# A fused low-rank update on one core: TensorE's program written as one loop, the turned group at a fixed place, last loads of 8 and 4 tiles

## The chip, the core and the metric

The kernel runs on one core of one Trainium2 chip. The core has TensorE (PE, matrix products), VectorE (DVE), ScalarE (ACT), GpSimd (POOL) and SyncE (SP, which here only issues DMAs and passes signals on). Data moves between the chip's memory (HBM) and the core's memory (SBUF) by DMAs, which 16 DMA engines of the core carry out together. Matrix products land in PSUM. The metric is the time of one execution on the device, in microseconds (us); lower is better.

## The reference

```
batch, seq, d_model, r = 16, 512, 768, 16
x: [16, 512, 768] f32    A: [768, 16]    B: [16, 768]    scale = 0.5

lora = np.matmul(np.matmul(x, A), B)
return (x + scale * lora).astype(np.float32)
```

As a matrix, x has 8192 rows of 768. The inner dimension of the update is 16, so there is little arithmetic, while all of x is read (25.2 MB) and a result of the same size is written.

## The kernel before

**Tiles, groups, parts.** A tile is 128 rows of x by 768, and there are 64. All of them stay in SBUF in one buffer, `x_all`, and the sums are written in place there. Four tiles are a group (16 groups, 0 to 15); two tiles are a pair. The tiles lie in five parts of 8, 16, 16, 12 and 12 (`PARTS`). A part is stored by one DMA: stores 0 to 4 follow groups 1, 5, 9, 12 and 15. The loads are the list `LOADS` (part, first tile, tiles): loads 0 to 7 have 2, 6, 8, 8, 16, 12, 10 and 2 tiles. In `x_all` the last part's place also serves as room for the constants while they are prepared (`lent`), so loads 6 and 7, which fill that place, can only start when its lodgers are gone.

**The stages of a group g.**

1. *Narrowing* (L209 to L223): ScalarE copies two tiles of the group to 16 bit, GpSimd the other two. Group 1 is narrowed whole by ScalarE.
2. *Turning* (L276 to L278): VectorE transposes the narrowed group in blocks of 32x32.
3. *Projecting* (L312 to L327): 24 matmuls on TensorE multiply by A, in a block-diagonal form `w_bd`. The second raises `s_taken`, the last raises `s_y`.
4. *Spreading* (L261 to L265): ScalarE multiplies the small result by the scale and writes it into a block-diagonal `y_bd`, of which there are two.
5. *Raising* (L329 to L345): 8 matmuls multiply by B (`b_mm`), four for each pair of tiles, into two PSUM buffers `lora`.
6. *Summing* (L280 to L287): VectorE adds the PSUM buffer to `x_all`, one instruction for a pair.

**Places.** The narrowed group lies in one fixed buffer `xn` (group 1: in lent room, `xn_1`). The turned group moves (`turn_of`, L106): the last two tiles' place of `x_all` for groups 0 and 2 to 7 (`xt_a`), lent room for group 1 (`xt_1`), in place in `xn` for groups 8 to 10 (`PLACE`), and from group 11 on the first two tiles' place, `xt_c`, which is free once store 0 has landed (`s_out0`).

**Orders.** Each engine has its own program, and semaphores tie them together.

- TensorE (L347 to L383): it first copies B to four row blocks (L349 to L353), then projects groups 0 and 1, then for each g: raise g, project g + 2. Because the address of the turned group changes, the `while` loop (L368) writes this as a hardware loop of three passes for g = 0 to 5, four steps written out, a loop of two passes, and the last two raises written out. As the program's order lists them, 322 matmuls stand in it; 514 are executed.
- VectorE (L289 to L307): turn 0, turn 1, then for each g: turn g + 2, sum the two pairs of g.
- ScalarE (L254 to L267): narrow, make `b_mm`, then for each g: spread g, narrow its half of g + 2.
- GpSimd (L225 to L252): clears buffers, prepares `w_bd`, then narrows its halves.
- SyncE (L181 to L207): loads 0 and 1, A, B, loads 2 to 5; waits for the first raise (`s_lora`) and issues load 6; waits for the sums of parts 0 and 1 and for the projection of group 7 (`s_y`, L200) and issues load 7; waits until load 6 has landed (L202) and issues stores 0 and 1; then waits for the sums of each further part and issues its store. All these DMAs go through one queue, q1.

Of the kernel before, what the change touches and what calls it, by code (L numbers as in the profile page):

```python
# [9 lines left out]
MM_DT = mybir.dt.float16  # L10
# [3 lines left out]
PARTS = [8, 16, 16, 12, 12]  # L14


GROUP = 4

SUB = 2
# [2 lines left out]


PLACE = range(8, 11)

APART = 4
# [4 lines left out]
def kernel(  # L34
# [9 lines left out]
    fp32 = mybir.dt.float32  # L44
    P = 128
    Q = 32
    NQ = P // Q
# [3 lines left out]
    T, D = x2.shape  # L51
    R = A.shape[1]
    NC = D // 64
    NG = sum(PARTS) // GROUP
    PAIRS = GROUP // 2
# [4 lines left out]
    def sb(name, shape, dtype):  # L60
        return nc.alloc_sbuf_tensor(name, shape, dtype).ap()
# [6 lines left out]
    ROOM = sum(PARTS)  # L68
    x_all = sb("x_sb", [P, ROOM, D], fp32)
    w_bd = sb("w_bd", [P, NC, 2, P], MM_DT)  # L70
    b_mm = sb("b_mm", [P, D], MM_DT)
    xn = sb("xn", [P, GROUP, D], MM_DT)
    y_bd = sb("y_bd", [P, 2, GROUP, P], MM_DT)
    lora = [ps(f"lora_ps{i}", [P, 2, D]) for i in range(2)]
    y_ps = [ps(f"ps_yt{i}", [P, GROUP, Q]) for i in range(2)]
# [5 lines left out]
    def lent(n, dtype=fp32):  # L81
        n = n if dtype is fp32 else n // 2
        taken[0], first = taken[0] + n, taken[0]
        assert taken[0] <= (PARTS[-1] - SUB) * D
        v = late[:, ds(first, n)]
        return v if dtype is fp32 else v.bitcast(dtype)

# [3 lines left out]
    b_half = lent(D, MM_DT)  # L91
    pick = lent(P, MM_DT).rearrange("p (b r) -> p b r", b=NQ)
    w_one = lent(NC * 2 * R, MM_DT)[0:Q].rearrange("i (c k r) -> i c k r", c=NC, k=2)
    xn_1 = lent(GROUP * D, MM_DT).rearrange("p (s d) -> p s d", s=GROUP)
    xt_1 = lent(GROUP * D, MM_DT).rearrange("p (s d) -> p s d", s=GROUP)

    def turned_in(t):
        v = x_all[:, ds(t, SUB), :].rearrange("p s d -> p (s d)").bitcast(MM_DT)
        return v.rearrange("p (s d) -> p s d", s=GROUP)

    xt_a, xt_c = turned_in(ROOM - SUB), turned_in(0)

    def narrow_of(g):
        return xn_1 if g == 1 else xn

    def turn_of(g):  # L106
        return xt_1 if g == 1 else xt_a if g < PLACE[0] else xn if g in PLACE else xt_c

    sems = []

    def sem(name):
        sems.append(nc.alloc_semaphore(name))
        return sems[-1]
# [17 lines left out]
    def tiles(t, n):  # L131
        return x_all[:, ds(t % ROOM, n), :]

    LOADS = [
        (0, 0, 2), (0, 2, 6), (1, 0, 8), (1, 8, 8), (2, 0, 16), (3, 0, 12), (4, 0, 10), (4, 10, 2)
    ]
    s_load = [sem(f"s_load{k}") for k in range(len(LOADS))]

# [6 lines left out]
    s_ready, s_brows, s_pick = sem("s_ready"), sem("s_brows"), sem("s_pick")  # L145
    s_wv = sem("s_wv")
    s_w, s_bh, s_bp, s_bm = sem("s_w"), sem("s_bh"), sem("s_bp"), sem("s_bm")
    s_first, s_narrow, s_taken = sem("s_first"), sem("s_narrow"), sem("s_taken")
    s_turned = [sem(f"s_turned{h}") for h in range(2)]
    s_y, s_spread, s_lora = sem("s_y"), sem("s_spread"), sem("s_lora")  # L150


    s_free = [[sem(f"s_free{h}_{p}") for p in range(PAIRS)] for h in range(2)]
# [12 lines left out]
    def on_sync(e):  # L166
        def load(k):
            ld = LOADS[k]
            e.dma_start(out=held(*ld), in_=memory(x2, *ld)).then_inc(s_load[k], 16)

        def summed(k):
            e.wait_ge(s_sum, k + 1)
            if STORED[k] + 1 < NG:

                e.sem_inc(s_free[STORED[k] % 2][PAIRS - 1], 1)

        def store(k, done):
            st = STORES[k]
            e.dma_start(out=memory(out2, *st), in_=held(*st)).then_inc(done, 16)

        load(0)  # L181
        load(1)
        e.wait_ge(s_ready, 1)
        blocks = A.rearrange("(c e) r -> c (e r)", e=64)
        for c in range(SETS):
            e.dma_start(  # L186
                out=a_rows[c : SET * SET : SET, :], in_=blocks[ds(c * SET, SET), :]
            ).then_inc(s_a, 16)
        e.wait_ge(s_brows, 1)
        e.dma_start(out=b_rows[0 : R * APART : APART, :], in_=B).then_inc(s_b, 16)  # L190
        for k in range(2, len(LOADS) - 2):
            load(k)

        for p in range(PAIRS):
            e.sem_inc(s_free[1][p], 1)
        e.wait_ge(s_lora, 1)
        load(len(LOADS) - 2)
        summed(0)
        summed(1)
        e.wait_ge(s_y, PLACE[0])  # L200
        load(len(LOADS) - 1)
        e.wait_ge(s_load[len(LOADS) - 2], 16)  # L202
        store(0, s_out0)
# [7 lines left out]
    def narrowed(e, copy, g, first, n=SUB):  # L211
        t = g * GROUP + first
        for k in dict.fromkeys(load_of(t + k) for k in range(n)):
            if (e, k) not in here:
                here.add((e, k))
                e.wait_ge(s_load[k], 16)
        if g - 1 in PLACE:
            e.wait_ge(s_y, g)
        elif g > 1:
            e.wait_ge(s_taken, g if g > 2 else 1)  # L220
        ins = copy(out=narrow_of(g)[:, ds(first, n), :], in_=tiles(t, n))  # L221

        ins.then_inc(s_narrow if g > 1 else s_first if g or first else s_a, 1)  # L223

    def on_gpsimd(e):  # L225
        e.memset(a_rows[0:Q], 0.0).then_inc(s_ready, 1)  # L226
# [19 lines left out]
        for b in range(NQ - 1):  # L246
# [4 lines left out]
        for g in range(2, NG):  # L251
            narrowed(e, e.tensor_copy, g, SUB)  # L252

    def on_scalar(e):  # L254
        narrowed(e, e.copy, 0, SUB)
        narrowed(e, e.copy, 1, 0, GROUP)
        e.wait_ge(s_bp, 1)
        e.copy(out=b_mm, in_=lora[0][:, 0, :]).then_inc(s_bm, 1)
        narrowed(e, e.copy, 2, 0)
        for g in range(NG):  # L260
            e.wait_ge(s_y, g + 1)  # L261
            for b in range(NQ):
                q = ds(b * Q, Q)
                last = e.mul(out=y_bd[q, g % 2, :, q], in_=y_ps[g % 2][q, :, :], mul=sc)  # L264
            last.then_inc(s_spread, 1)  # L265
            if 1 <= g < NG - 2:
                narrowed(e, e.copy, g + 2, 0)  # L267

    def on_vector(e):
        e.wait_ge(s_a, SETS * 16 + 1)  # L270
        e.transpose(  # L271
            out=a_t[0:Q].rearrange("i k r c -> i (k r) c"),
            in_=a_rows[0:Q].rearrange("c (i k r) -> c (k r) i", k=2, r=R),
        ).then_inc(s_ready, 1)

        def turned(g):  # L276
            ts = [v.bitcast(fp32) for v in (turn_of(g), narrow_of(g))]
            e.transpose(out=ts[0], in_=ts[1]).then_inc(s_turned[g % 2], 1)  # L278

        def summed(g, p):  # L280
            xs = tiles(g * GROUP + 2 * p, 2)
            e.wait_ge(s_lora, g * PAIRS + p + 1)
            ins = e.tensor_tensor(out=xs, in0=xs, in1=lora[p % 2], op=mybir.AluOpType.add)  # L283
# [5 lines left out]
        for g in range(2):  # L289
            e.wait_ge(s_first, g + 1)  # L290
            turned(g)
            if g == 0:
                b = NQ - 1
                e.wait_ge(s_w, 1)
                e.tensor_copy(
                    out=w_bd[ds(b * Q, Q), :, :, ds(b * Q, R)], in_=w_one
                ).then_inc(s_wv, 1)
        for g in range(NG):
            if g + 2 < NG:
                if g + 2 == PLACE[-1] + 1:  # L300
                    e.wait_ge(s_out0, 16)
                elif g + 2 not in PLACE:
                    e.wait_ge(s_y, g + 2 if g else 1)
                e.wait_ge(s_narrow, 2 * (g + 1))
                turned(g + 2)
            for p in range(PAIRS):
                summed(g, p)  # L307

    def on_tensor(e):


        def projected(h, xt):  # L312
# [15 lines left out]

        def raised(h, p):  # L329
            if p == 0:  # L330
                e.wait_ge(s_spread, 1)
            free = s_free[1 - h][p]
            e.wait_ge(free, 1)
            t = lora[p % 2]
# [5 lines left out]
                        start=True, stop=True,  # L340
                    ))
            if p == 0:
                mms[2].then_inc(s_spread, -1)
            mms[1].then_inc(free, -1)
            mms[-1].then_inc(s_lora, 1)  # L345

# [7 lines left out]
        last.then_inc(s_bp, 1)  # L354
        e.wait_ge(s_w, NQ)
        e.wait_ge(s_wv, 1)
        projected(0, turn_of(0))
        projected(1, turn_of(1))
        e.wait_ge(s_bm, 1)

        def step(g):
            for p in range(PAIRS):
                raised(g % 2, p)
            if g + 2 < NG:
                projected(g % 2, turn_of(g + 2))

        g = 0
        while g < NG:  # L368

            n = 1  # L370
            while g + 2 * n + 3 < NG and all(
                turn_of(t + 2) is turn_of(g + 2) for t in range(g, g + 2 * n + 2)
            ):
                n += 1
            same = g + 3 < NG and turn_of(g + 2) is turn_of(g + 3)
            if same and n > 1 and g % 2 == 0:
                with e.Fori(0, n):
                    step(g)
                    step(g + 1)
                g += 2 * n  # L380
            else:
                step(g)
                g += 1  # L383

    on_sync(nc.sync)
    on_gpsimd(nc.gpsimd)
# [47 lines left out]
```

## Time and profile before

| what | value |
|---|---|
| median of 3 runs | 125.72 us (125.69 to 125.72) |
| the profiled execution's own time | 125.75 us |
| its span | 124.0 us, so 1.75 us of its time lie outside the span |
| mean granted TensorE clock | 0.88 of full speed |
| moved by DMA | 50.48 MB, 407 GB/s over the span |
| busy shares | VectorE 67%, TensorE 45%, ScalarE 35%, GpSimd 24% |

How to read it: a busy share is an engine's busy time over the span. In the view of DMA queues, a row gives the queue, its packets, the MB they moved and the time they took as a share of 16 engines times the length of the stretch asked for. A packet is counted in the stretch in which it *starts*, with all the time it took; in a short stretch the share can so be over 100%, and for a single packet share x length x 16 gives how long that packet took. At the end of each load and store, every DMA engine sends one packet of 4 bytes that signals its own part as done; the count "under 512 B" so shows when each of the 16 engines came to the end of a transfer.

### The profile page before, as it was taken

To read this page: it belongs to the slowest core of one execution; us is meant where nothing else is said; L and a number is where in the kernel's file an instruction comes from. 1 tells how busy PE (TensorE), PEld (TensorE's weight loads), DVE (VectorE), ACT (ScalarE), POOL (GpSimd) and SP (SyncE) were. 2 spreads that over 40 slices of the span, in tenths; PEclk is the share of its full clock that TensorE was granted. 3 is DMA by queue.
4 is the path that set the end of the run, shared out by engine and by line. 5 is a ranking of instruction groups with operands and counts; after the bars stand their busy time and mean duration, and the time that the engine had idled before them with its cause. 6 is when DMAs were issued, how large, how long until landed. Compare 5 with 4: busy or idle time off the path is not lost.

```text
span 124.0 us, 1339 instructions
## 1 busy us (share of the span) xinstructions
PE 55.5 (45%) x514; PEld 36.5 (29%) x514; DVE 82.8 (67%) x50; ACT 43.9 (35%) x82; POOL 29.2 (24%) x30
## 2 busy tenths in 40 slices
PE   0000287947647249947647249757647520000000
PEld 0000086634415046534415044534515200000000
DVE  0003954999999099999999199999999991000000
ACT  4003929827430555716174334726533000000000
POOL 7722604404400421404044031413400000000000
PEclk9999999999999955999999985999999998555555
DMA  3999999999899899899699999699799999999980
GB/s 67 436 416 468 420 428 444 412 492 508 354 397 448 381 500 452 379 416 466 266 389 494 397 508 460 291 508 476 333 460 494 416 393 393 404 512 416 404 381 12
DMA packets 1932, 50.48 MB, mean 407 GB/s; under 512 B 236, under 2 KB 236, under 8 KB 520
## 3 DMA queue, kind: packets, MB, share of 16 engines
q1 hardware_dynamic: 1928, 50.43, 95.4%
q8 instruction: 2, 0.03, 0.1%
q14 instruction: 2, 0.02, 0.0%
HBM read 25.26 MB, written 25.17 MB: 407 GB/s over the span
## 4 chain that ended last, share of the span: by engine, by line
DMA 51%; DVE 22%; issue 4%; SPq 2%; ACT 2%; POOL 1%; PE 1%; POOLq 0%
DMA x_sb<-in_x_dram 43%; DVE x_sb L283 15%; DMA out_dram<-x_sb 8%; DVE x_sb L278 7%; SPq L186 2%; ACT xn L221 1%; ACT y_bd L264 1%; POOL x_sb L226 1%; PE lora_ps L338 1%; SPq L190 0%; POOLq L429 0%; SPq L164 0%
## 5 line engine op out<-in xcount | busy, mean ns | idle before, releaser
L283 DVE TENSOR_TENSOR x_sb<-x_sb,lora_ps 128x1536 f32<-128x1536 f32 x32 | 54.0, 1732 | 0.0
L221 ACT CAST xn<-x_sb 128x1536 f16<-128x1536 f32 x15 | 22.1, 1472 | 45.0 <-PE ps_yt L317 27.1
L221 POOL CAST xn<-x_sb 128x1536 f16<-128x1536 f32 x15 | 22.0, 1466 | 54.1 <-PE ps_yt L317 43.0
L338 PE MATMUL lora_ps<-b_mm,y_bd 128*128 128x512 f16 (+1 forms) x128 | 27.7, 346 | 12.9 <-DVE x_sb L283 8.6
L317 PE MATMUL ps_yt<-x_sb,w_bd 128*128 128x128 f16 x312 | 23.1, 237 | 16.4 <-DVE x_sb L278 13.8
L317 PEld LDWEIGHTS ps_yt<-x_sb,w_bd 128*128 128x128 f16 x312 | 21.3, 105 | 20.8 <-issue 20.6
L278 DVE STREAM_TRANSPOSE x_sb<-xn 128x1536 f32<-128x1536 f32 x12 | 21.2, 1763 | 8.6 <-PE ps_yt L317 3.1
L264 ACT ACTIVATE y_bd<-ps_yt 32x128 f16<-32x128 f32 x64 | 17.2, 268 | 5.8 <-PE ps_yt L317 4.9
L338 PEld LDWEIGHTS lora_ps<-b_mm,y_bd 128*128 128x128 f16 x128 | 11.0, 102 | 26.1 <-DVE x_sb L283 11.5
L271 DVE STREAM_TRANSPOSE x_sb<-x_sb 32x1024 f32<-32x1024 f32 x1 | 1.9, 1948 | 11.3 <-DMA x_sb<-in_A_dram 11.3
L350 PE MATMUL lora_ps<-x_sb 128*128 128x512 f16 (+1 forms) x2 | 0.8, 504 | 12.5 <-POOL x_sb L239 12.5
L317 PE MATMUL ps_yt<-xn,w_bd 128*128 128x128 f16 x72 | 4.6, 218 | 3.0 <-DVE xn L278 3.0
L317 PEld LDWEIGHTS ps_yt<-xn,w_bd 128*128 128x128 f16 x72 | 4.2, 96 | 4.0 <-issue 4.0
L278 DVE STREAM_TRANSPOSE xn<-xn 128x1536 f32<-128x1536 f32 x3 | 5.3, 1772 | 0.0
L350 PEld LDWEIGHTS lora_ps<-x_sb 128*128 128x128 f16 x2 | 0.1, 104 | 12.5 <-issue 12.5
L221 ACT CAST x_sb<-x_sb 128x3072 f16<-128x3072 f32 x1 | 2.7, 2746 | 0.0
L239 POOL CAST x_sb<-x_sb 128x768 f16<-128x768 f32 x1 | 0.8, 827 | 4.6 <-DMA x_sb<-in_B_dram 4.6
L278 DVE STREAM_TRANSPOSE x_sb<-x_sb 128x1536 f32<-128x1536 f32 x1 | 1.8, 1778 | 0.0
L221 ACT ACT_TABLE_LOAD x1 | 1.3, 1283 | 0.9 <-SPq L164 0.9
L247 POOL COPY w_bd<-x_sb 32x384 f16<-32x384 f16 x3 | 1.5, 499 | 0.2
L229 POOL MEMSET w_bd<- 128x1536 f32 x1 | 1.4, 1372 | 0.0
L226 POOL MEMSET x_sb<- 32x1024 f32 x1 | 0.9, 942 | 0.5 <-SPq L164 0.5
(11 smaller groups left out, 4.2 us busy)
## 6 DMA issues: line engine op xcount, KB each, us to landing
out_dram<-x_sb SPq DMA_DIRECT2D x2, 6144.0 KB, 25.0
out_dram<-x_sb SPq DMA_DIRECT2D x2, 4608.0 KB, 20.6
x_sb<-in_x_dram SPq DMA_DIRECT2D x2, 3072.0 KB, 17.4
x_sb<-in_x_dram SPq DMA_DIRECT2D x1, 6144.0 KB, 35.9
x_sb<-in_x_dram SPq DMA_DIRECT2D x1, 4608.0 KB, 46.4
x_sb<-in_x_dram SPq DMA_DIRECT2D x1, 3840.0 KB, 39.6
out_dram<-x_sb SPq DMA_DIRECT2D x1, 3072.0 KB, 9.4
x_sb<-in_x_dram SPq DMA_DIRECT2D x1, 2304.0 KB, 9.8
```

Of the source, the lines that this page charges most:

```text
L186: e.dma_start(out=a_rows[c : SET * SET : SET, :], in_=blocks[ds(c * SET, SET), :]).then_inc(s_a, 16)
L221: ins = copy(out=narrow_of(g)[:, ds(first, n), :], in_=tiles(t, n))
L226: e.memset(a_rows[0:Q], 0.0).then_inc(s_ready, 1)
L229: e.memset(w_bd.rearrange("p c k m -> p (c k m)").bitcast(fp32), 0.0)
L247: e.tensor_copy(out=w_bd[ds(b * Q, Q), :, :, ds(b * Q, R)], in_=w_one).then_inc(s_w, 1)
L264: last = e.mul(out=y_bd[q, g % 2, :, q], in_=y_ps[g % 2][q, :, :], mul=sc)
L271: e.transpose(out=a_t[0:Q].rearrange("i k r c -> i (k r) c"), in_=a_rows[0:Q].rearrange("c (i k r) -> c (k r) i", k=2, r=R),).then_inc(s_r ...
L278: e.transpose(out=ts[0], in_=ts[1]).then_inc(s_turned[g % 2], 1)
L283: ins = e.tensor_tensor(out=xs, in0=xs, in1=lora[p % 2], op=mybir.AluOpType.add)
L317: mm = e.matmul(y_ps[h], w_bd[:, c, k, :], xv[:, :, c, :, k], start=(m == 0), stop=(m == MMS - 1),)
L338: mms.append(e.matmul(t[:, k, ds(n0, w)], y_bd[:, h, 2 * p + k, :], b_mm[:, ds(n0, w)], start=True, stop=True,))
L350: last = e.matmul(lora[0][:, 0, ds(n0, w)], pick.rearrange("p b r -> p (b r)"), b_half[:, ds(n0, w)], start=True, stop=True,)
```

## The change

The narrowed group and the turned group change roles. The turned group has one fixed buffer, `xt`, in all groups. The narrowed group moves (`narrow_of`): the last two tiles' place of `x_all` for groups 0 to 7 (`xn_a`), `xt` itself for groups 8 to 10 (turned in place), and the first two tiles' place from group 11 on (`xn_c`). With it:

- The lent buffers `xn_1` and `xt_1` are gone. Group 1 is narrowed half by ScalarE, half by GpSimd like the others, after group 0's projection has begun.
- The waits for a place stand at the narrowing: groups 8 to 10 wait for the projection before (`s_y`), group 11 waits until store 0 has landed, the others wait for `s_taken`. Every turn but the first waits for the projection before it.
- TensorE's program is one hardware loop of eight passes: project an even group, raise the group before, project an odd group, raise the group before; one raise follows the loop. In the first pass the raise before group 0 works on a cleared `y_bd`, and nobody reads what it writes. SyncE opens the semaphores that this empty raise waits for; counts of `s_lora` are two higher. 74 matmuls stand in the program; 522 are executed. TensorE now waits for `b_mm` ahead of group 0's projection.
- `s_narrow` and `s_spread` are split in two, for even and odd groups.
- Loads 6 and 7 have 8 and 4 tiles. Load 6 waits for the third count of `s_lora`, load 7 for `s_taken` of group 7 in place of its `s_y`.

```diff
-    xt_a, xt_c = turned_in(ROOM - SUB), turned_in(0)
+    xn_a, xn_c = narrow_in(ROOM - SUB), narrow_in(0)
 
     def narrow_of(g):
-        return xn_1 if g == 1 else xn
-
-    def turn_of(g):
-        return xt_1 if g == 1 else xt_a if g < PLACE[0] else xn if g in PLACE else xt_c
+        return xn_a if g < PLACE[0] else xt if g in PLACE else xn_c
...
-        (0, 0, 2), (0, 2, 6), (1, 0, 8), (1, 8, 8), (2, 0, 16), (3, 0, 12), (4, 0, 10), (4, 10, 2)
+        (0, 0, 2), (0, 2, 6), (1, 0, 8), (1, 8, 8), (2, 0, 16), (3, 0, 12), (4, 0, 8), (4, 8, 4)
...
-        for p in range(PAIRS):
-            e.sem_inc(s_free[1][p], 1)
-        e.wait_ge(s_lora, 1)
+        for h in range(2):
+            for p in range(PAIRS):
+                e.sem_inc(s_free[h][p], 1)
+        e.sem_inc(s_spread[1], 1)
+        e.wait_ge(s_lora, PAIRS + 1)
         load(len(LOADS) - 2)
         summed(0)
         summed(1)
-        e.wait_ge(s_y, PLACE[0])
+        e.wait_ge(s_taken, PLACE[0])
         load(len(LOADS) - 1)
...
-        if g - 1 in PLACE:
+        if g in PLACE:
             e.wait_ge(s_y, g)
-        elif g > 1:
-            e.wait_ge(s_taken, g if g > 2 else 1)
+        elif g == PLACE[-1] + 1:
+            e.wait_ge(s_out0, 16)
+        elif g:
+            e.wait_ge(s_taken, g)
...
         narrowed(e, e.copy, 0, SUB)
-        narrowed(e, e.copy, 1, 0, GROUP)
         e.wait_ge(s_bp, 1)
         e.copy(out=b_mm, in_=lora[0][:, 0, :]).then_inc(s_bm, 1)
-        narrowed(e, e.copy, 2, 0)
+        narrowed(e, e.copy, 1, 0)
...
+        for t in range(1, NG + 2):
+            if t < NG:
+                e.wait_ge(s_y, t)
+                e.wait_ge(s_narrow[t % 2], 2 * ((t + 1) // 2))
+                turned(t)
+            if t > 1:
+                for p in range(PAIRS):
+                    summed(t - 2, p)
...
-        projected(0, turn_of(0))
-        projected(1, turn_of(1))
         e.wait_ge(s_bm, 1)
...
+        with e.Fori(0, NG // 2):
+            for h in range(2):
+                projected(h)
+                for p in range(PAIRS):
+                    raised(1 - h, p)
+        for p in range(PAIRS):
+            raised(1, p)
```

More of the change, by code (lines that the diff above doesn't have):

```diff
@@ L71 @@
     b_mm = sb("b_mm", [P, D], MM_DT)
-    xn = sb("xn", [P, GROUP, D], MM_DT)
+    xt = sb("xt", [P, GROUP, D], MM_DT)
     y_bd = sb("y_bd", [P, 2, GROUP, P], MM_DT)
@@ L83, in lent @@
         taken[0], first = taken[0] + n, taken[0]
-        assert taken[0] <= (PARTS[-1] - SUB) * D
+        assert taken[0] <= (PARTS[-1] - GROUP) * D
         v = late[:, ds(first, n)]
@@ L93, with narrow_in @@
     w_one = lent(NC * 2 * R, MM_DT)[0:Q].rearrange("i (c k r) -> i c k r", c=NC, k=2)
-    xn_1 = lent(GROUP * D, MM_DT).rearrange("p (s d) -> p s d", s=GROUP)
-    xt_1 = lent(GROUP * D, MM_DT).rearrange("p (s d) -> p s d", s=GROUP)
-    def turned_in(t):
+    def narrow_in(t):
         v = x_all[:, ds(t, SUB), :].rearrange("p s d -> p (s d)").bitcast(MM_DT)
         return v.rearrange("p (s d) -> p s d", s=GROUP)
-    xt_a, xt_c = turned_in(ROOM - SUB), turned_in(0)
+    xn_a, xn_c = narrow_in(ROOM - SUB), narrow_in(0)
     def narrow_of(g):
-        return xn_1 if g == 1 else xn
-    def turn_of(g):
-        return xt_1 if g == 1 else xt_a if g < PLACE[0] else xn if g in PLACE else xt_c
+        return xn_a if g < PLACE[0] else xt if g in PLACE else xn_c
     sems = []
@@ L147 @@
     s_w, s_bh, s_bp, s_bm = sem("s_w"), sem("s_bh"), sem("s_bp"), sem("s_bm")
-    s_first, s_narrow, s_taken = sem("s_first"), sem("s_narrow"), sem("s_taken")
+    s_first, s_taken = sem("s_first"), sem("s_taken")
+    s_narrow = [sem(f"s_narrow{h}") for h in range(2)]
     s_turned = [sem(f"s_turned{h}") for h in range(2)]
-    s_y, s_spread, s_lora = sem("s_y"), sem("s_spread"), sem("s_lora")
+    s_y, s_lora = sem("s_y"), sem("s_lora")
+    s_spread = [sem(f"s_spread{h}") for h in range(2)]
     s_free = [[sem(f"s_free{h}_{p}") for p in range(PAIRS)] for h in range(2)]
@@ L216, in narrowed @@
                 e.wait_ge(s_load[k], 16)
-        if g - 1 in PLACE:
+        if g in PLACE:
             e.wait_ge(s_y, g)
-        elif g > 1:
-            e.wait_ge(s_taken, g if g > 2 else 1)
+        elif g == PLACE[-1] + 1:
+            e.wait_ge(s_out0, 16)
+        elif g:
+            e.wait_ge(s_taken, g)
         ins = copy(out=narrow_of(g)[:, ds(first, n), :], in_=tiles(t, n))
-        ins.then_inc(s_narrow if g > 1 else s_first if g or first else s_a, 1)
+        ins.then_inc(s_narrow[g % 2] if g else s_first if first else s_a, 1)
     def on_gpsimd(e):
@@ L250, in on_gpsimd @@
             e.wait_ge(s_w, b + 2)
-        for g in range(2, NG):
+        for g in range(1, NG):
             narrowed(e, e.tensor_copy, g, SUB)
@@ L264, in on_scalar @@
                 last = e.mul(out=y_bd[q, g % 2, :, q], in_=y_ps[g % 2][q, :, :], mul=sc)
-            last.then_inc(s_spread, 1)
-            if 1 <= g < NG - 2:
+            last.then_inc(s_spread[g % 2], 1)
+            if g + 2 < NG:
                 narrowed(e, e.copy, g + 2, 0)
@@ L276, in turned @@
         def turned(g):
-            ts = [v.bitcast(fp32) for v in (turn_of(g), narrow_of(g))]
+            ts = [v.bitcast(fp32) for v in (xt, narrow_of(g))]
             e.transpose(out=ts[0], in_=ts[1]).then_inc(s_turned[g % 2], 1)
@@ L281, in summed @@
             xs = tiles(g * GROUP + 2 * p, 2)
-            e.wait_ge(s_lora, g * PAIRS + p + 1)
+            e.wait_ge(s_lora, (g + 1) * PAIRS + p + 1)
             ins = e.tensor_tensor(out=xs, in0=xs, in1=lora[p % 2], op=mybir.AluOpType.add)
@@ L287, in summed, with projected @@
                 ins.then_inc(s_free[g % 2][p], 1)
[L289 to L307, printed above, removed]
+        e.wait_ge(s_first, 1)
+        turned(0)
+        b = NQ - 1
+        e.wait_ge(s_w, 1)
+        e.tensor_copy(
+            out=w_bd[ds(b * Q, Q), :, :, ds(b * Q, R)], in_=w_one
+        ).then_inc(s_wv, 1)
+        for t in range(1, NG + 2):
[6 more added lines that the diff above has]
+                    summed(t - 2, p)
     def on_tensor(e):
-        def projected(h, xt):
+        def projected(h):
             xv = xt.rearrange("p s (c j k) -> p s c j k", c=NC, k=2)
@@ L330, in raised @@
             if p == 0:
-                e.wait_ge(s_spread, 1)
+                e.wait_ge(s_spread[h], 1)
             free = s_free[1 - h][p]
@@ L342, in raised @@
             if p == 0:
-                mms[2].then_inc(s_spread, -1)
+                mms[2].then_inc(s_spread[h], -1)
             mms[1].then_inc(free, -1)
@@ L356, in on_tensor @@
         e.wait_ge(s_wv, 1)
-        projected(0, turn_of(0))
-        projected(1, turn_of(1))
         e.wait_ge(s_bm, 1)
[L361 to L383, printed above, removed]
+        with e.Fori(0, NG // 2):
[5 more added lines that the diff above has]
+            raised(1, p)
     on_sync(nc.sync)
```

## The prediction

> **What bounds the kernel now.** I read the page first: engines, DMA queues, the chain and the DMA issues.
>
> ```profile
> span 124.0 us, 1339 instructions
> PE 55.5 (45%) x514; PEld 36.5 (29%) x514; DVE 82.8 (67%) x50; ACT 43.9 (35%) x82; POOL 29.2 (24%) x30
> ...
> DMA packets 1932, 50.48 MB, mean 407 GB/s; under 512 B 236, under 2 KB 236, under 8 KB 520
> ...
> q1 hardware_dynamic: 1928, 50.43, 95.4%
> q8 instruction: 2, 0.03, 0.1%
> q14 instruction: 2, 0.02, 0.0%
> out_dram<-x_sb SPq DMA_DIRECT2D x2, 4608.0 KB, 20.6
> ```
>
> The DMA engines work 95.4% of the span in q1; VectorE, the busiest engine, works 67%. Then SyncE's timeline over the whole span, and VectorE's last row there:
>
> ```profile
> 61.65 41.44 SPq L179 DMA_DIRECT2D out_dram<-x_sb  x5
> 92.69 10.04 DVE L283 TENSOR_TENSOR x_sb<-x_sb,lora_ps 128x1536 f32<-128x1536 f32 x6
> ```
>
> The sums end at 102.73, and the last store is issued right then (61.65 + 41.44 = 103.09 is the end of that issue). It needs some 20 us to land, since the two stores of 4608 KB take 20.6 in the middle, though their data alone need 4.72 MB / 407 GB/s = 11.6. So it stands in the queue for about 9 us: the compute is early, and the time is the DMA engines' time. What counts is where they stand idle and which of the 16 is last. The first is in the windows at 61.4 (columns: window, length, VectorE busy, TensorE clock, DMA share, GB/s):
>
> ```profile
> 61.40:62.40 1.00, 1.00 (x2) 1.00 0.15 61
> 62.40:63.40 1.00, 0.98 (x2) 1.00 0.97 406
> ```
>
> In one microsecond they move 61 GB/s in place of 406, so 0.85 us is lost. The chain of waits and the view of DMA queues, asked for the stretches 59 to 60.2, 60.2 to 61.1 and 61.15 to 61.2, tell why:
>
> ```profile
> 22.01 39.62 DMA x_sb<-in_x_dram
> 61.65 9.37 DMA out_dram<-x_sb
> ```
>
> ```profile
> DMA packets 60, 0.30 MB, mean 251 GB/s; under 512 B 15, under 2 KB 15, under 8 KB 59
> ```
>
> ```profile
> DMA packets 58, 0.36 MB, mean 396 GB/s; under 512 B 0, under 2 KB 0, under 8 KB 58
> ```
>
> ```profile
> DMA packets 4, 0.02 MB, mean 369 GB/s; under 512 B 1, under 2 KB 1, under 8 KB 4
> ```
>
> Load 6 lands at 22.01 + 39.62 = 61.63 and store 0 is issued at 61.65 (L202). But 15 of the 16 engines had closed load 6 by 60.2 (15 small packets); the last one does so at 61.15 to 61.2, about 1 us later. The 15 then have only load 7 left, 2 tiles, or 0.79 MB / 407 GB/s = 1.9 us, and run dry before store 0 reaches them.
>
> The second place is the end, in the same view from 120.7 to 121.2, 121.2 to 121.6, 121.6 to 122 and 122 to 122.7:
>
> ```profile
> DMA packets 12, 0.00 MB, mean 0 GB/s; under 512 B 12, under 2 KB 12, under 8 KB 12
> ```
>
> ```profile
> DMA packets 2, 0.04 MB, mean 92 GB/s; under 512 B 1, under 2 KB 1, under 8 KB 1
> ```
>
> ```profile
> DMA packets 2, 0.00 MB, mean 0 GB/s; under 512 B 2, under 2 KB 2, under 8 KB 2
> ```
>
> ```profile
> DMA packets 1, 0.00 MB, mean 0 GB/s; under 512 B 1, under 2 KB 1, under 8 KB 1
> ```
>
> Twelve engines are done by 121.2, then one, two, and a last one after 122; from the last two packets' places I put it at 122.6, some 1.5 us behind the twelve.
>
> What makes one engine late? The instruction queues, q8 and q14. In the view of queues, the stretches 32.3 to 32.4, 33.3 to 33.4, then 75.4 to 75.405, 77.7 to 77.9, 78.7 to 78.8, and at last 95 to 96.5:
>
> ```profile
> q1 hardware_dynamic: 4, 0.20, 450.4%
> q8 instruction: 1, 0.02, 65.6%
> ```
>
> ```profile
> q1 hardware_dynamic: 1, 0.05, 145.1%
> ```
>
> ```profile
> q1 hardware_dynamic: 1, 0.05, 3016.2%
> ```
>
> ```profile
> q8 instruction: 1, 0.02, 30.0%
> ```
>
> ```profile
> q1 hardware_dynamic: 1, 0.05, 136.6%
> ```
>
> ```profile
> q14 instruction: 1, 0.01, 1.3%
> ```
>
> An ordinary packet of 49 KB takes 4.504 x 1.6 / 4 = 1.80 us. The q8 packet at 32.3 takes 0.656 x 1.6 = 1.05, and the data packet that begins when it ends takes 1.451 x 1.6 = 2.32, so 0.52 too long: one engine loses 1.57 at most, and about 1 us is what load 6's last engine lacks. The q8 packet at 77.8 takes 0.300 x 3.2 = 0.96, with a data packet ahead of 30.162 x 0.08 = 2.41 and one behind of 1.366 x 1.6 = 2.19: 0.96 + 0.61 + 0.39 = 1.96 lost on one engine, about the 1.5 by which the last engine is late. That these packets hit just these engines is my inference; the sizes and the times fit.
>
> **The change, part by part.** *Instructions.* 322 matmuls, each with its weight load, stand in TensorE's program now, and 74 then. The others execute 82 (ScalarE), 50 and 30 instructions, so only TensorE's program is long enough to be fetched twice in blocks of q8's size; I take q8 to be its. A program of under a quarter of the length needs no second fetch, or one. Value: the late one goes, the early one may stay. Bounds: both stay (0), both go.
>
> The Trainium skill (Runtime: NRT & Kernel Launch, Instruction fetch mechanics) says that programs are fetched in blocks of 16 KiB by the sequencer's own queue; the trace agrees, with q8's 0.03 MB in 2 packets. By it 2 x 74 instructions, at 256 to a block, would fit one block, and both packets would go: an end at 121.1, and the same sum.
>
> *Last loads.* Load 6 has 8 tiles in place of 10, so it lands 2 x 0.393 MB / 407 GB/s = 1.9 us earlier, at 59.7 even with its late engine. Behind it load 7 has 3.9 us of work in place of 1.9; both together end where they did, so the first engines still run dry at about 61.4, and store 0, issued 1.9 us earlier, is there by then (the row at 62.40 shows it at work 0.75 us after its issue). The idle 0.85 us goes, for each engine but the late one. That one had none, and was among the twelve that end by 121.2 (the hole gave the others its delay).
>
> *The sum.* Ends now: twelve by 121.2, the others at about 121.5, 122, 122 and 122.6. Without the hole the ordinary ones end by 120.3 and the two of 122 at 121.1; those I leave late, since q14's packet (0.013 x 1.5 x 16 = 0.31 and its neighbours) lies in that stretch and belongs to programs that hardly change. If the early q8 packet stays, its engine ends at 121.2. The last end goes from 122.6 to 121.1 or 121.2 (120.8 if the two come out a little better): 1.4 to 1.8 less, and I take 1.7. 125.75 - 1.7 = 124.05, rounded to **124.0**; the median of the runs shown, 125.72, is the same within 0.03.
>
> *The start.* TensorE's timeline, then VectorE's, ScalarE's and VectorE's again:
>
> ```profile
> 15.90 4.35 PE L317 MATMUL ps_yt<-x_sb,w_bd 128*128 128x128 f16 x48 [2.58 <-POOL w_bd L247]
> ...
> 21.16 1.47 PE L338 MATMUL lora_ps<-b_mm,y_bd 128*128 128x512 f16 x8 [0.91 <-ACT y_bd L264]
> ...
> 47.66 2.49 PE L338 MATMUL lora_ps<-b_mm,y_bd 128*128 128x512 f16 x8
> ```
>
> ```profile
> 20.28 1.78 DVE L278 STREAM_TRANSPOSE x_sb<-xn 128x1536 f32<-128x1536 f32 x1 [3.12 <-PE ps_yt L317]
> ```
>
> ```profile
> 41.62 1.47 ACT L221 CAST xn<-x_sb 128x1536 f16<-128x1536 f32 x1 [6.44 <-DMA x_sb<-in_x_dram]
> ```
>
> ```profile
> 43.22 1.78 DVE L278 STREAM_TRANSPOSE x_sb<-xn 128x1536 f32<-128x1536 f32 x1 [2.82 <-POOL xn L221]
> ```
>
> Group 1 now follows group 0: its narrowing begins once group 0's projection has (15.9 + 0.4), ends at 17.8, its turn waits for that projection's end (15.9 + 2.2 = 18.1) and ends at 19.9; the empty raise (8 matmuls, 1.47 to 2.49 us by the rows at 21.16 and 47.66) lies beside it. Projection 1 starts at about 20.2, group 2 is narrowed from 20.6 to 22.1 and turned at 22.1, in place of 20.28: 1.8 us late. At 43.22 VectorE now waits 2.82 us for group 6, whose load lands at 41.62; the delay is swallowed there, with 1.0 us to spare. Without this cover, it would come out of the 9 us that the last store stands in the queue.
>
> Load 7 is issued behind the sums of group 5; SyncE's timeline has it at
>
> ```profile
> 53.39 0.33 SPq L169 DMA_DIRECT2D x_sb<-in_x_dram  x1
> ```
>
> a stretch that the delay doesn't reach; it must be there by 59. The other groups keep the order turn, sum, sum at 5.0 us a group. Groups 8 to 10 are narrowed one projection (1.5 us) later and still end when VectorE comes free, as groups 9 to 11 do now. `b_mm` comes earlier than `w_bd`, so its new place costs nothing.
>
> *Group 11.* Its turn waits for store 0 now:
>
> ```profile
> 71.04 1.78 DVE L278 STREAM_TRANSPOSE x_sb<-xn 128x1536 f32<-128x1536 f32 x1 [2.63 <-DMA out_dram<-x_sb]
> ```
>
> After the change the narrowing waits for it, so the turn comes 1.5 us (one CAST of 1.47) later, and all that follows on VectorE with it. Behind the wait on ScalarE stands the spreading of group 10, on GpSimd nothing that is due; the raise of group 10 comes after projection 11 anyway. The last store is issued at 104.3 in place of 102.8. The stretch 109 to 112.5 shows all 16 engines closing store 3:
>
> ```profile
> DMA packets 52, 1.33 MB, mean 379 GB/s; under 512 B 16, under 2 KB 16, under 8 KB 16
> ```
>
> So store 4 is wanted from 109 on at the earliest, 108.15 without the hole; less 0.75 for the way from issue to work, there are 3.1 us to spare. Stores 2 and 3, behind the sums of groups 9 and 12, have as much or more. Cost: nothing, up to that bound.
>
> **The rivals.**
>
> 1. *Only the hole goes.* A late instruction packet stays (TensorE's, or one of the tail's) and one engine ends 2 us behind the ordinary ones: 120.3 + 1.5 to 2.0 = 121.8 to 122.3, so 125.0. For it: q8's owner is inferred. Or the hole stays and the late packet goes: 122 in place of 122.6, 125.1.
> 2. *Nothing.* The early and the late packet both stay and meet on one engine. The early one's engine ends by 121.2 though it never idled; the late loss of 1.5 to 1.96 on top gives 122.6 or a little more: 125.7.
> 3. *Slower: the loop fetches itself again.* The loop is jumped back to seven times. If each pass fetched a block, 8 packets of q8 at 1.57 to 1.96 would fall on the 16 engines; it decides once two of them meet on one engine late: 120.3 + 2 x 1.96 = 124.2, or 127.3 in all; all eight on one would give 135. Against it: the program now makes five passes in two loops, and q8 shows two packets. The Trainium skill says at the same place that a taken branch out of the two pages held forces a fetch before execution goes on; of that these rows show nothing.
>
> **How the numbers follow.** Forecast (both terms, 123.6 to 124.5): 0.60. Rival 1: 0.20. Rival 2: 0.06. Rival 3, 0.10, and with it any compute delay of more than the 3.1 us to spare at store 4. Better still (all late engines in line, 120.3, so 123.4 and below): 0.04. The forecast and rival 1 hold 0.80: the range is 123.4 to 125.2. Within 0.2% (0.25 us, about what a measurement of this kernel can tell from no change): 0.06; faster 0.84; slower 0.10.
>
> **What would show it.** Right: no q8 row, or one early; GB/s near 406 through 59 to 63; store 0 issued before 60; the last of the small packets near 121; group 11's turn 1 to 1.5 us behind store 0's landing, the last sum near 104. Wrong: several q8 packets, a new stretch of few GB/s behind store 0, 3 or 4 (the sums are late), or a last engine 2 us behind the rest.

## The result, and the profile after

The changed kernel takes 123.91 us (median; 123.87 to 124.01) against 125.70 for the kernel before beside it: a ratio of 0.9861, 95% interval 0.9844 to 0.9878. 124.0 had been forecast. The profiled execution took 123.87 us, 1.88 less than that of before, and its span went from 124.0 to 122.1. The page of the changed kernel, in the lines that answer to those of before:

```profile
span 122.1 us, 1371 instructions
PE 56.6 (46%) x522; PEld 37.0 (30%) x522; DVE 82.8 (68%) x50; ACT 42.8 (35%) x82; POOL 30.7 (25%) x31
...
DMA packets 1930, 50.45 MB, mean 413 GB/s; under 512 B 236, under 2 KB 236, under 8 KB 392
...
q1 hardware_dynamic: 1928, 50.43, 96.7%
q14 instruction: 2, 0.02, 0.0%
...
out_dram<-x_sb SPq DMA_DIRECT2D x1, 3072.0 KB, 11.4
```

The same data moves in less time, and no row for q8 is left: both of TensorE's 16 KB packets are gone, not only the late one. The windows of the changed kernel at the place of the hole (window, length, VectorE busy, clock, DMA share, GB/s) show 516 GB/s where there were 61:

```profile
61.40:62.40 1.00, 1.00 (x1) 0.50 1.21 516
62.40:63.40 1.00, 0.56 (x1) 0.50 1.14 492
```

SyncE's timeline of the changed kernel over the whole span gives the issue of load 7, and then the five stores, the first at 58.69 in place of 61.65:

```profile
52.84 0.33 SPq L164 DMA_DIRECT2D x_sb<-in_x_dram  x1
58.69 45.11 SPq L174 DMA_DIRECT2D out_dram<-x_sb  x5
```

The view of DMA queues of the changed kernel, for the stretches 57.4 to 58.3 (load 6), and then 119.3 to 119.9, 119.9 to 120.5 and 120.5 to 120.8 (store 4); the count under 512 B is that of the engines that close the transfer:

```profile
DMA packets 39, 0.28 MB, mean 314 GB/s; under 512 B 16, under 2 KB 16, under 8 KB 16
...
DMA packets 14, 0.04 MB, mean 62 GB/s; under 512 B 13, under 2 KB 13, under 8 KB 13
...
DMA packets 1, 0.00 MB, mean 0 GB/s; under 512 B 1, under 2 KB 1, under 8 KB 1
...
DMA packets 2, 0.00 MB, mean 0 GB/s; under 512 B 2, under 2 KB 2, under 8 KB 2
```

All 16 engines close load 6 within 0.9 us; before, one was a microsecond behind. At the end 13 are done by 119.9 and the last by 120.8, where 12 had been done by 121.2 and the last after 122. VectorE in the changed kernel's timeline, at groups 2, 6, 10, 11 and the last sums:

```profile
22.72 1.78 DVE L277 STREAM_TRANSPOSE xt<-x_sb 128x1536 f32<-128x1536 f32 x1 [2.13 <-POOL x_sb L221]
...
42.69 1.76 DVE L277 STREAM_TRANSPOSE xt<-x_sb 128x1536 f32<-128x1536 f32 x1
...
63.96 1.78 DVE L277 STREAM_TRANSPOSE xt<-xt 128x1536 f32<-128x1536 f32 x1 [1.00 <-POOL xt L221]
...
71.74 1.78 DVE L277 STREAM_TRANSPOSE xt<-x_sb 128x1536 f32<-128x1536 f32 x1 [2.69 <-POOL x_sb L221]
...
93.39 10.04 DVE L282 TENSOR_TENSOR x_sb<-x_sb,lora_ps 128x1536 f32<-128x1536 f32 x6
```

VectorE starts later, turns group 11 at 71.74 in place of 71.04 and ends at 103.43 in place of 102.73, in a kernel that is 1.8 us faster: the compute does not set the time.

### The profile page after: what moved, and what is told of

It reads as the page before. It is cut to its first block, busy times and chain, and to the rows that moved or that the text cites. A ratio compares the mean times of both kernels' runs of the same rounds, so it can differ in the third digit from the quotient of the medians.

```text
span 122.1 us, 1371 instructions
## 1 busy us (share of the span) xinstructions
PE 56.6 (46%) x522; PEld 37.0 (30%) x522; DVE 82.8 (68%) x50; ACT 42.8 (35%) x82; POOL 30.7 (25%) x31
## 4 chain that ended last, share of the span: by engine, by line
DMA 45%; DVE 25%; issue 5%; PE 4%; POOL 4%; SPq 1%; POOLq 0%; DVEq 0%
DMA x_sb<-in_x_dram 29%; DVE x_sb L282 15%; DMA out_dram<-x_sb 9%; DVE xt L277 9%; DMA x_sb<-in_A_dram 6%; PE ps_yt L312 3%; DVE x_sb L270 2%; POOL w_bd L247 1%; POOL x_sb L221 1%; SPq L181 1%; POOL x_sb L226 1%; POOL x_sb L241 1%; PE lora_ps L333 1%; POOLq L406 0%; DVEq L298 0%
## 5 line engine op out<-in xcount | busy, mean ns | idle before, releaser
L312 PE MATMUL ps_yt<-xt,w_bd 128*128 128x128 f16 x384 | 27.8, 233 | 19.7 <-DVE xt L277 17.0
L333 PE MATMUL lora_ps<-b_mm,y_bd 128*128 128x512 f16 (+1 forms) x136 | 28.7, 340 | 12.2 <-DVE x_sb L282 8.6
L312 PEld LDWEIGHTS ps_yt<-xt,w_bd 128*128 128x128 f16 x384 | 25.2, 103 | 25.7 <-issue 25.7
L221 ACT CAST x_sb<-x_sb 128x1536 f16<-128x1536 f32 x13 | 19.1, 1472 | 35.9 <-PE ps_yt L312 18.9
L221 POOL CAST x_sb<-x_sb 128x1536 f16<-128x1536 f32 x13 | 19.1, 1468 | 40.3 <-PE ps_yt L312 29.2
L277 DVE STREAM_TRANSPOSE xt<-x_sb 128x1536 f32<-128x1536 f32 x13 | 22.9, 1763 | 8.3 <-POOL x_sb L221 4.8
L333 PEld LDWEIGHTS lora_ps<-b_mm,y_bd 128*128 128x128 f16 x136 | 11.8, 102 | 25.3 <-DVE x_sb L282 11.7
L221 ACT CAST xt<-x_sb 128x1536 f16<-128x1536 f32 x3 | 4.4, 1472 | 9.6 <-PE ps_yt L312 9.6
L221 POOL CAST xt<-x_sb 128x1536 f16<-128x1536 f32 x3 | 4.4, 1469 | 13.0 <-PE ps_yt L312 13.0
L277 DVE STREAM_TRANSPOSE xt<-xt 128x1536 f32<-128x1536 f32 x3 | 5.3, 1778 | 1.1 <-POOL xt L221 1.0
## 6 DMA issues: line engine op xcount, KB each, us to landing
x_sb<-in_x_dram SPq DMA_DIRECT2D x1, 6144.0 KB, 34.8
out_dram<-x_sb SPq DMA_DIRECT2D x1, 3072.0 KB, 11.4
```

Source lines behind the costliest of these rows:

```text
L312: mm = e.matmul(y_ps[h], w_bd[:, c, k, :], xv[:, :, c, :, k], start=(m == 0), stop=(m == MMS - 1),)
L333: mms.append(e.matmul(t[:, k, ds(n0, w)], y_bd[:, h, 2 * p + k, :], b_mm[:, ds(n0, w)], start=True, stop=True,))
```

## The experiments

The theory: two terms. One late DMA engine keeps load 6 open, so store 0 is issued late and the others run dry (the hole); and one engine ends late. Both come from TensorE's instruction packets in q8. The rivals: the loads' sizes alone, the loop alone, or a time that follows VectorE.

| kernel | q8 packets | time, us | ratio to before, 95% interval |
|---|---|---|---|
| before | 2 | 125.70 to 125.79 | 1 |
| changed | 0 | 123.91; 124.01 when run again | 0.9861 [0.9844, 0.9878]; 0.9859 [0.9842, 0.9877] |
| before, loads 8 and 4 | 2 | 124.36 | 0.9884 [0.9867, 0.9900] |
| changed, loads 10 and 2 | 0 | 124.05 | 0.9858 [0.9841, 0.9874] |
| changed, passes written out | 4 | 124.47 | 0.9896 [0.9880, 0.9913] |
| changed, two passes written out | 1 | 124.29 | 0.9890 [0.9868, 0.9911] |
| changed, written out, loads 10 and 2 | 4 | 126.06 | 1.0025 [1.0014, 1.0036] |
| before, no wait for load 6 | 2 | 125.32 | 0.9950 [0.9934, 0.9967] |
| before, store 0 ahead of that wait | 2 | 125.17 | 0.9943 [0.9924, 0.9963] |
| changed, no wait for load 6 | 0 | 124.35 | 0.9889 [0.9873, 0.9906] |
| changed, two more turns | 0 | 124.13 | 0.9868 [0.9844, 0.9893] |
| changed, four more turns | 0 | 125.61 | 0.9988 [0.9974, 1.0001] |

### The last loads alone, in the kernel before

```diff
-        ... (4, 0, 10), (4, 10, 2)
+        ... (4, 0, 8), (4, 8, 4)
```

> The kernel before, with last loads of 8 and 4 tiles and nothing else of the change. Theory (two terms: a hole behind load 6, and a late engine through TensorE's instruction packets): the hole goes, the two q8 packets stay. The ordinary engines close store 4 about 1.2 to 1.4 us earlier than before (near 119.5 to 119.9), the engine of the late q8 packet near 121.4, so a span about 1.2 shorter and a time of 124.4 to 124.7. Rival A (the loads do it all, the instruction packets cost nothing): 123.9, as with the whole change. Rival B (the loads do nothing, the program's length does it all): 125.7.

124.36. Queues of this kernel over the span, its window at the place of the hole, then the queue view for 119.4 to 120.6, 120.6 to 121 and 121 to 121.6:

```profile
q8 instruction: 2, 0.03, 0.1%
...
61.40:62.40 1.00, 1.00 (x2) 1.00 1.10 467
...
DMA packets 15, 0.11 MB, mean 92 GB/s; under 512 B 12, under 2 KB 12, under 8 KB 12
...
DMA packets 1, 0.00 MB, mean 0 GB/s; under 512 B 1, under 2 KB 1, under 8 KB 1
...
DMA packets 3, 0.00 MB, mean 0 GB/s; under 512 B 3, under 2 KB 3, under 8 KB 3
```

The hole is gone: 467 GB/s where there were 61, and the ordinary engines end about as early as in the changed kernel. Rival B falls by the time. Against rival A the time alone says little: the loads alone leave some 0.4 us, by the medians, that the whole change gains, but the intervals overlap. The trace says more. One engine still lags at load 6: 15 close it from 57.5 to 58.5, the last between 59.7 and 59.9. At store 4 the last engine closes 1.7 us behind the middle of the 16, their median (121.52 and 119.85), in the changed kernel 1.1 (120.67 and 119.58). This profile is of the slowest of the four runs (124.60).

### The loop and the places alone, in the changed kernel

```diff
-        ... (4, 0, 8), (4, 8, 4)
+        ... (4, 0, 10), (4, 10, 2)
```

> The changed kernel, with last loads of 10 and 2 tiles as before: the loop and the new places alone. Theory: without an early q8 packet no engine lags at load 6, so it closes on all engines by about 60.2, store 0 is issued near 60.6 and at work near 61.4, when the first engines run dry: a hole of 0.1 us or less, no late engine, 123.9 to 124.1. Rival (the hole is there in any case with a load 7 of 2 tiles): 0.85 to 1.2 us more, 124.7 to 125.1.

124.05, as the theory had it: with no q8 packet no engine lags far behind at load 6 (all 16 close it from 59.2 to 60.5), and there is next to no hole, though load 7 has 2 tiles as before. Its windows at the place, and the queue view for 120 to 120.6 and 121 to 121.2:

```profile
60.40:61.40 1.00, 1.00 (x2) 1.00 1.00 412
61.40:62.40 1.00, 1.00 (x1) 1.00 1.12 467
62.40:63.40 1.00, 1.00 (x2) 1.00 0.93 393
...
DMA packets 14, 0.00 MB, mean 0 GB/s; under 512 B 14, under 2 KB 14, under 8 KB 14
...
DMA packets 2, 0.00 MB, mean 0 GB/s; under 512 B 2, under 2 KB 2, under 8 KB 2
```

The hole was not a matter of the 2-tile load alone: it needs the late engine too. The end is not quite what the theory had. The profile is of the slowest of the four runs (124.33), and in it two engines close store 4 after 121, some 0.9 us behind the rest, with no q8 packet at all. The changed kernel has two such engines as well (120.5 to 120.8). So not every late engine at the end is due to q8, and a count of engines that end after 121 proves little by itself.

### All passes written out

```diff
-        with e.Fori(0, NG // 2):
+        for _ in range(NG // 2):
```

> The changed kernel with TensorE's eight passes written out (522 matmuls in the program) in place of the loop. Theory: q8 comes back with 3 or 4 packets of 16 KB; each costs its engine 1.5 to 2 us; on engines of their own the last one closes near 121.3 in place of 120.7, or 121.6 where it carries a small q14 packet too: 124.4 to 124.9; where two meet on one engine, 126 to 126.5. No hole, since load 7 has 4 tiles. Rival (the instruction packets are hidden, the gain came from the hole alone): 123.9.

124.47. The queue view of this kernel over the span, and for 121 to 121.4:

```profile
q8 instruction: 4, 0.07, 0.2%
...
DMA packets 4, 0.00 MB, mean 0 GB/s; under 512 B 4, under 2 KB 4, under 8 KB 4
```

Four packets are back with TensorE's longer program, which settles whose they are; four engines end after 121, no hole opens (its windows stand in the next experiment), and 0.5 us is lost.

The Trainium skill (Runtime: NRT & Kernel Launch, Instruction fetch mechanics) gives 256 instructions to a block of 16 KiB. That agrees: counting a matmul and its weight load as two, the programs have about 148, 404, 644 and 1044 instructions, and q8 shows 0, 1, 2 and 4 packets, one for each whole block of 256. The same section calls the cost of a block mostly hidden; for TensorE it was (it waited 16.6 us for VectorE's turns here, 17.0 with the loop), but not for the DMA engine that carried it.

### Written out, with loads of 10 and 2 tiles

```diff
+        ... (4, 0, 10), (4, 10, 2)
...
+        for _ in range(NG // 2):
```

> The changed kernel with TensorE's eight passes written out and the last loads of 10 and 2 tiles. With all passes written out, two q8 packets of 16 KB came before load 6 closed, on two engines. Theory: they make load 6 close 1 to 1.4 us late, and with a load 7 of only 2 tiles the other engines run dry: a hole of 0.9 to 1.2 us is back. The late engines of the second half get it on top: 124.47 + 0.9 to 1.2 = 125.3 to 125.7. Rival (the hole belongs to the old places and their order, not to the packets): none, 124.4 to 124.7.

126.06: slower than the kernel before, by more than I expected. Its windows at the place of the hole:

```profile
60.40:61.40 1.00, 1.00 (x2) 1.00 0.88 363
61.40:62.40 1.00, 1.00 (x2) 1.00 0.24 98
62.40:63.40 1.00, 1.00 (x2) 1.00 1.02 430
```

The hole is back with all of the new places and orders kept, so it belongs to the packets and the short load 7: 14 engines close load 6 by 60, the other two only after 61. The same windows of the kernel written out with loads of 8 and 4:

```profile
60.40:61.40 1.00, 1.00 (x1) 1.00 1.08 455
61.40:62.40 1.00, 1.00 (x2) 1.00 1.01 430
62.40:63.40 1.00, 1.00 (x1) 1.00 1.09 467
```

Each window is 1 us, so the three moved 363 + 98 + 430 = 891 KB against 1352: 461 KB are missing, 1.1 us at 413 GB/s. 1.6 us are lost in all. The rest is on the late engines: the middle of the 16 closes store 4 about 1.05 us later than with loads of 8 and 4 (121.16 for 120.11), the last one 1.54 later (122.83 for 121.29). Why the last ones lag more here stays open. Written out, the changed kernel is no faster than the kernel before with the same loads (124.47 to 124.36, and 126.06 to 125.78; it has four q8 packets to two), so nothing here shows a gain from the new places and orders by themselves.

### Two passes written out

```diff
-        with e.Fori(0, NG // 2):
+        with e.Fori(0, NG // 2 - 2):
...
+        for _ in range(2):
```

> The changed kernel with six passes in the loop and the last two written out (202 matmuls in the program). Theory: one q8 packet; where it falls in the second half it costs its engine about 1.9 us, and that engine closes store 4 near 121.4: 124.4 to 124.7; where it is fetched early, 1.0 to 1.6 us, and the engine is level with the two that are late anyway (120.7): 123.9 to 124.2. Rival (hidden): 123.9 with the packet in the second half.

124.29, with single runs from 123.97 to 124.69: between the two cases, and the interval overlaps that of the changed kernel, so the time decides nothing. The profile, which is of the quickest of these runs, shows more. The queue view for 83.1 to 83.3, 84.1 to 84.2 and 120.8 to 120.9:

```profile
q8 instruction: 1, 0.02, 31.8%
...
q1 hardware_dynamic: 2, 0.05, 139.5%
...
DMA packets 1, 0.00 MB, mean 0 GB/s; under 512 B 1, under 2 KB 1, under 8 KB 1
```

The packet takes 0.318 x 3.2 = 1.02 us and the data packet that follows on its engine 1.395 x 1.6 = 2.23 (with a packet of 4 bytes in it) in place of 1.8; the one ahead is not stretched. So it costs 1.4 us, not 1.9. In the trace each packet begins within 15 ns of the end of the one before it on its engine; followed in this way, the engine of the q8 packet is the one that closes store 4 last, at 120.85, but only 0.25 us behind the next and not at 121.4. What the three slower runs had more, no profile shows.

### No wait for load 6, before and after, and one store ahead of it

```diff
-        e.wait_ge(s_load[len(LOADS) - 2], 16)
         store(0, s_out0)
```

> The kernel before without SyncE's wait for load 6 ahead of store 0 (store 0 reads nothing of load 6); the instructions of the other engines, the loads of 10 and 2 tiles and the old places stay. Theory: store 0 stands in the queue behind load 7 in good time, the hole is gone although the early q8 packet stays, and the time is that of the kernel before with loads of 8 and 4: 124.3 to 124.6. Rival A (the hole is no waiting for the issue but a change from reading to writing): it stays, 125.7. Rival B (loads of 8 and 4 helped through their sizes): 125 and more.

125.32: not what the theory had, and not rival A. It lies where rival B put it, but the sizes of the loads are not what counts: the loop alone takes 124.05 with loads of 10 and 2. I then tried the same in the changed kernel, and in the kernel before store 0 alone ahead of the wait, store 1 behind it:

> The changed kernel without SyncE's wait for load 6 ahead of store 0. It has no hole to lose. Theory from the kernel before without that wait (its load packets between 58 and 61 became slow as soon as two stores stood queued behind them): the same happens here, 0.5 to 1 us more, 124.4 to 124.9. Rival (that slowness belongs to the old places or to the 2-tile load): 123.9.

> The kernel before with store 0 issued ahead of the wait for load 6 and store 1 behind it. If one store queued early is harmless: the hole is gone and the late packets stay, 124.3 to 124.6. If a store queued early behind the loads is what slows their packets: 125.2 to 125.4, as without the wait. If the hole is no matter of waiting for the issue: 125.7.

```diff
-        e.wait_ge(s_load[len(LOADS) - 2], 16)
         store(0, s_out0)
+        e.wait_ge(s_load[len(LOADS) - 2], 16)
```

124.35 and 125.17; the changed kernel, unedited beside them, 124.01:

> The changed kernel itself, beside the others of this call on one chip: 123.9.

The queue view of the kernel without the wait, from 60.4 to 61.2, and of the kernel before, from 60.2 to 61.1; nearly all packets are of load 7, 6 KB each:

```profile
DMA packets 30, 0.18 MB, mean 230 GB/s; under 512 B 0, under 2 KB 0, under 8 KB 30
...
q1 hardware_dynamic: 30, 0.18, 73.1%
```

```profile
q1 hardware_dynamic: 58, 0.36, 95.7%
```

The hole is gone, but in this stretch a packet of load 7 takes 0.731 x 12.8 / 30 = 0.31 us in place of 0.957 x 14.4 / 58 = 0.24, and the load ends later: 15 engines close it by 62.7, before by 61.9. One store queued early is enough for that (125.17). The changed kernel seems to lose by it too: 0.34 us beside it, with intervals that just overlap, and all 16 engines close load 7 from 61.6 to 62.5 in place of 61.1 to 61.95.

The slowness does not last as long as the stores stand there. They are issued at 53.9. From 54 to 57 the packets of load 6 take 1.14 us with them and without (42 packets at 100.0%, 38 at 90.4%, of 48 us), and from 61.2 to 61.8 those of load 7 take 0.24 again (39 at 96.5% of 9.6 us). Between lie about two slow microseconds, from 59 to 61, in all three kernels with an early store. Why, these runs don't show.

So the wait for load 6 is not simply a waste. In the kernel before, it still costs more than it saves: without it the kernel is 0.46 us faster (125.32 against 125.78). In the changed kernel, which has no hole, nothing speaks for taking it out.

### Two and four more turns of group 11

```diff
+            for k in range(2 if g == PLACE[-1] + 1 else 0):
+                e.transpose(out=ts[0], in_=ts[1]).then_inc(s_again, 1)
+                e.wait_ge(s_again, k + 1)
             e.transpose(out=ts[0], in_=ts[1]).then_inc(s_turned[g % 2], 1)
```

> The changed kernel with the turn of group 11 done three times in place of once, one after the other: VectorE is 3.6 us later from there on. The last store is wanted at 108.5 less 0.75 and is issued at 103.5 in the changed kernel: 4.3 us to spare. Theory (compute has slack, the DMA engines set the time): 123.9, last store issued near 107.1. Rival (the time follows VectorE): 127.5.

> The changed kernel with the turn of group 11 done five times: VectorE is 7.2 us later from there on. Theory: 4.3 us are covered, 2.9 us come out, spread over holes ahead of stores 2, 3 and 4: 126.6 to 127.0. [...] Rival (time follows VectorE fully): 131.

124.13, hidden, with VectorE's last row (of the kernel with two more) at

```profile
96.92 10.04 DVE L285 TENSOR_TENSOR x_sb<-x_sb,lora_ps 128x1536 f32<-128x1536 f32 x6
```

so the last sum ends at 106.96. With four, 125.61: 1.6 to 1.7 us come out where I had 2.9. Its queue view from 122.3 to 122.5 tells where the rest went:

```profile
DMA packets 16, 0.00 MB, mean 0 GB/s; under 512 B 16, under 2 KB 16, under 8 KB 16
```

All 16 engines close store 4 within 0.2 us. The middle of the 16 closes stores 2, 3 and 4 later than in the changed kernel by 1.7, 2.1 and 2.8 us (99.49, 110.83 and 122.40 for 97.81, 108.69 and 119.58), at the end about as worked out; the last one, by 120.8 there, only 1.7. In the holes ahead of the stores the late engines catch up: the last one lags 0.9 us behind the middle at store 2, 0.5 at store 3 and 0.1 at store 4, and this lag is no longer paid. Holes and late engines do not add up.

## Why the prediction was right

- **The bound.** Right: the DMA engines. Two more turns, 3.6 us on VectorE from group 11 on, cost 0.1 to 0.2 us, about the spread of the changed kernel's runs.
- **The hole.** The mechanism was right and shown from both sides: it needs one engine late at load 6 and a load 7 of 2 tiles. Take either away and it is gone (124.36, 124.05); put both back into the changed kernel, and it is back (126.06). Its size was taken too small: 0.85 us from one window, outside of which its edges lie. The middle of the 16 engines closes store 0 at 69.91 before and at 68.81 after, 1.1 us earlier, and store 4 about 1.3 earlier (120.92 and 119.58); the last 0.2 stay open.
- **The late engine.** Right as well: q8's packets are TensorE's, and the engine that lags is the one that carries them, which had been inferred. The queue view of the kernel before for 24.7 to 25.5 (the end of load 3), 39.2 to 40.1 and 40.1 to 41.2 (the end of load 4, during which the early q8 packet comes at 32.3), then of the changed kernel for 39.2 to 40.1:

```profile
DMA packets 32, 0.79 MB, mean 983 GB/s; under 512 B 16, under 2 KB 16, under 8 KB 16
...
DMA packets 31, 0.60 MB, mean 669 GB/s; under 512 B 15, under 2 KB 15, under 8 KB 15
...
DMA packets 13, 0.44 MB, mean 402 GB/s; under 512 B 1, under 2 KB 1, under 8 KB 1
```

```profile
DMA packets 32, 0.59 MB, mean 655 GB/s; under 512 B 16, under 2 KB 16, under 8 KB 16
```

  Nobody lags before the packet, one engine by over a microsecond behind it, and nobody in the kernel without it. The late packet (77.8) does the same in store 1: 15 engines close it from 84.3 to 85.1, one after that. With the hole out of play the packets cost 0.4 us (two) to 0.5 (four) by the medians; the four are clear of the changed kernel's interval, the two overlap it a little. My 1.96 for the late one was what that engine lost, not what the kernel loses: two engines stay late by about 1 us anyway (120.5 to 120.8), which I had left in the sum.
- **The early packet.** "May stay" was the cautious choice; it went, and the loads came earlier for it: load 4 lands 34.8 to 35.2 us behind its issue in the kernels with no q8 packet before it (the changed one, loads of 10 and 2, two passes written out), 35.9 to 36.4 with one (before, the loads alone, both written out). ScalarE's timeline of the changed kernel has group 6's narrowing, which waits for load 4, at

```profile
40.47 1.47 ACT L221 CAST x_sb<-x_sb 128x1536 f16<-128x1536 f32 x1 [2.93 <-DMA x_sb<-in_x_dram]
```

  in place of 41.62. So VectorE had no wait left at group 6, and yet was there earlier (42.69 for 43.22).
- **The sum.** 1.7 forecast, 1.79 by the medians. The sum's own terms, 122.6 down to 121.1, are 1.5: 0.85 for the hole and 0.65 for the late engine. In the profiled executions the last closing went from 122.64 to 120.67: 1.34 for the middle of the engines, and 0.64 less lag of the last one behind it. So the late engine was sized well and the hole 0.5 us too small; that 1.7 was taken in place of 1.5 hid a part of this, and that the total came so near is partly luck. The parts don't add as the prediction lets one think: the loads alone bring 1.43 and the loop alone 1.74, since each removes the hole, and only what is left after it belongs to one of them. The loop alone is as good as the whole change within the intervals.
- **The start.** Right in kind, 0.6 us short: the turn of group 2 came at 22.72, not 22.1, since projection 0 took 2.71 us, not half of a row of 48 matmuls (4.35). Its cover held.
- **Groups 8 to 10.** I had them free; group 10 made VectorE wait 1.00 us, with the clock at 0.50 in that stretch. Hidden, like group 11 (store 0 lands at 58.69 + 11.4 = 70.1, the turn comes 1.6 us later at 71.74, and the last sum ends at 103.43, where 104 was expected).
- **The rivals.** The first, in which only the hole goes, is the kernel with the loads alone: it takes 124.36, not 125.0. (Its ends of 121.8 to 122.3 would give 124.95 to 125.45, so it was not wholly inside the range.) A loop that fetches itself again (0.10): none in seven jumps back. Its worst case was mis-added: 120.3 + 8 x 1.57, with the 3.15 us from the last closing to the time, is 136, not 135. Of the Trainium skill's rule that a branch out of the two pages held forces a fetch (Runtime: NRT & Kernel Launch, same section) no run here shows anything: with a program of under one block, no fetch came at all.

## What to carry to other kernels

Where the DMA engines set the time, look at each of the 16 for itself: count the small closing packets in a short stretch, and a transfer that is late on one engine shows at once. A wait for a transfer to land is a wait for the slowest engine, so what stands in the queue behind it must be longer than that engine's delay plus the way of the next issue (before, 1.3 us from the last engine's closing at 61.2 to the first packets of store 0 at 62.5; 2 tiles were too little and 4 enough); and a written-out program costs DMA time, as its blocks travel on the same engines as the data.

## What the runs showed of the hardware that I had not expected

- An instruction packet costs its engine more than its own time: 1.02 us became 1.4, 0.96 became 1.96, since the data packets beside it are stretched.
- With a store queued early behind loads, the loads' packets ran slower for about two microseconds, 5 us behind the store's issue: 0.31 us in place of 0.24 for 6 KB. Before and after that they did not.
- Behind a hole all engines start together, and their packets are slower for a while. The queue view of the kernel before and of the changed one, both from 63.2 to 64, when all packets are of store 0 (24.6 KB):

```profile
q1 hardware_dynamic: 16, 0.39, 117.4%
```

```profile
q1 hardware_dynamic: 14, 0.34, 99.8%
```

  1.174 x 12.8 / 16 = 0.94 us behind the hole, 0.998 x 12.8 / 14 = 0.91 without it; from 66.2 on both are at 0.92. This is too little to explain more than some 0.1 us.
